# Row norms of the first block in one batch of four, weight maxima taken before the gain, constants emitted later

## The chip, the cores and the metric

The kernel runs on one core of a Trainium2 chip. The metric is the device time of one execution in microseconds (us), as the median of several runs. One profiled execution of the same kernel gives the trace that is read below.

Engine names: PE multiplies matrices, DVE is the vector engine, ACT the scalar engine (activations, copies with a scale), POOL the general engine, SP the queue from which all transfers are issued. Each engine works its instructions in a fixed order, one after the other, and waits where an operand isn't there.

## The reference, cut to what matters

```
h = rms_norm(x, norm_in)                    # x: 4096 and 1024 rows of 1024
z = h @ w_in                                # columns: Hyena 3*384 | q,k,v 3*384 | memory q 256 | gates 1024
u = short_conv3(z[:, :1152]); x0, x1, v = split(u); s = x1 * v
y_hyena = x0 * (long_conv(s, filter) + s * skip)
y_att   = dilated_attention(q, k, v)        # 6 heads, three windows
y_mem   = memory_attention(qm, mem)         # 4 heads, 256 memory rows, rms_norm(mem, mem_norm) @ w_mem_kv
x + (concat(y_hyena, y_att, y_mem) * silu(gates)) @ w_out
```

The gain `norm_in` is a factor per input column, so the kernel multiplies it into the rows of `w_in`, and `mem_norm` into the rows of the memory weights.

## The kernel before

**Numbers in two halves.** A float32 operand is split into a high half and a low half of 16 bits, and `mm3` (L278) makes one product of three matmuls: high by high, high by low, low by high. One product `zh` is 24 matmuls.

**Weights.** `wsplit` (L238) prepares a group of weight columns, 128 columns each: it loads a column tile `ws` (128x1024), multiplies it by the gain on POOL (L251), takes its largest absolute value on DVE (L252), spreads the maxima over the partitions (`peaks`, L222 to L229, small DVE steps), makes a power of two of them and its reciprocal `wsa` (L257 to L260), scales the tile into the high half on ACT (L263) and subtracts that from the scaled tile for the low half on DVE (L265, two pieces). The Hyena weights come in the groups (0), (3, 6), (1, 4, 7), (2, 5, 8), nine columns in six buffers; the weights of q, k, v and the memory queries come later in groups of 2, 2, 2, 2 and 3 columns in three buffers, while the Hyena products still run.

**Rows.** `norm_rows` (L350) loads four tiles `xt` of 128 rows, squares them on ACT with a running sum (L362), makes 1/sqrt of the mean for `batch` tiles at once (`nv` L364, `rsqrt` L205 to L209, with one step on ACT), scales each tile into its high half on ACT (L368) and makes the low half on DVE (L369). Four buffers hold the tiles. `prep_block` (L374) turns the halves into `hB`: block 0 by PE transposes (L385) with copies out by ACT (L389) and DVE (L387), later blocks by transfers that transpose (L381). `BATCH0 = 2` is the batch of block 0; later blocks take 4.

**The projection.** `hyena_proj` (L833) runs ten blocks of 512 rows, nine products each; two PSUM buffers hold `zh`. ACT copies each product out as `zb` (L879, two buffers) and makes `u` (L889), DVE adds two taps (L893), POOL multiplies x1 by v (L901). Block n+1 is normalised while the products of block n run. The generator `filters` is woven in: it emits `setup_late` (gains of the heads, their scales `gk`, `gsc`, `lsc`, the memory gain `g_mem`, the matrices `dft` and `cinv`), then the filter of the long convolution.

**What sets the order.** PE's order is the order of the code (`manual_schedule`, with the generators interleaved by due times). On ACT, DVE, POOL and SP a scheduler puts the instructions in order by priorities and modelled times, so an edit in one place can move what stands behind it there.

Of the kernel before, what the change touches and what calls it, by code (L numbers as in the profile page):

```python
# [12 lines left out]
F32 = mybir.dt.float32  # L13
# [9 lines left out]
P = 128  # L23
# [118 lines left out]
K_C, IDLE_1, IDLE_2, IDLE_3, IDLE_M = 1.35, (34000, 28000), (9000, 16000), 18000, 60000  # L142
K_A, IDLE_A, GATE_IDLE = 0.88, 20000, 0
LAG_I, WS_BUFS = 6, 6
MT, BATCH0 = 4, 2
MIX, K_Q = 0.1, 1.2
AHEAD = 2
XT, VLAG = 2, 4
# [33 lines left out]
class Layer:  # L182
# [52 lines left out]
            out=out.bitcast(I32), in_=m.bitcast(I32), scalar=0x7F800000, op=ALU.bitwise_and  # L235
        )

    def wsplit(self, pool, parts, S, gain=None, tag="ws", bufs=3):  # L238

        nc = self.nc
        n = len(parts)
        ws = []
        a = pool.tile([P, 4, 4], F32, tag=tag + "a", name="wsa", bufs=2)
        pk = self.peak(pool, tag)
        for j, (src, _, _) in enumerate(parts):
            w = pool.tile([P, KC, P], F32, tag=tag, name="ws", bufs=bufs)
            self.ld(w, src)
            if gain is not None:  # L250
                nc.gpsimd.tensor_tensor(out=w, in0=w, in1=gain.unsqueeze(2).to_broadcast([P, KC, P]), op=ALU.mult)  # L251
            nc.vector.tensor_reduce(  # L252
                out=pk[:, j:j + 1], in_=w, axis=AX.XY, op=ALU.max, apply_absolute_value=True
            )
            ws.append(w)
        pk = self.peaks(pool, pk, tag)
        nc.vector.tensor_scalar_max(a[:, 1, :n], pk[:, :n], 1e-30)  # L257
        self.pow2(a[:, 2, :n], a[:, 1, :n])
        nc.vector.tensor_scalar_mul(S, a[:, 2, :n], 1.0 / 16.0)
        nc.vector.reciprocal(a[:, 3, :n], S)  # L260
        for j, (_, dhi, dlo) in enumerate(parts):
            w = ws[j]
            nc.scalar.activation(out=dhi, in_=w, func=AF.Identity, scale=a[:, 3, j:j + 1])  # L263
            for k in range(0, KC, 4):
                nc.vector.scalar_tensor_tensor(  # L265
                    out=dlo[:, k:k + 4], in0=w[:, k:k + 4], scalar=a[:, 3, j:j + 1], in1=dhi[:, k:k + 4],
                    op0=ALU.mult, op1=ALU.subtract,
                )
# [19 lines left out]
    def setup(self):  # L288
        nc, c, x = self.nc, self.const, self.x
        self.ident = c.tile([P, P], F32, name="ident")  # L290
        make_identity(nc, self.ident)
        self.ident16 = c.tile([P, P], F16, name="ident16")
        nc.vector.tensor_copy(self.ident16, self.ident)
        self.ones = c.tile([P, P], F32, name="ones")
        nc.vector.memset(self.ones, 1.0)
        self.g_in = c.tile([P, KC], F32, name="g_in")
        self.ld(self.g_in, x["norm_in"][0].rearrange("(k p) -> p k", p=P))
        self.cinv = {}
        for i, (off, L) in enumerate(self.seqs):
            self.kmT[i] = c.tile([P, 2 * HM, NMEM], F16, name=f"kmT{i}")  # L300
            self.vm[i] = c.tile([P, 2, HM * E1 + HM * E], F16, name=f"vm{i}")
            self.rows[i] = self.dram.tile([L, ROW], F16, name=f"rows{i}")
            self.vrows[i] = self.dram.tile([L, VW], F16, name=f"vrows{i}")
            self.s_d[i] = self.dram.tile([3, P, L], F32, name=f"s_d{i}")
            self.x0_d[i] = self.dram.tile([3, P, L], F32, name=f"x0_d{i}")
            self.cv[i] = self.dram.tile([3, P, L], F32, name=f"cv{i}")
            NB = 2 * L // N1
            G = -(-65 // (P // (2 * NB)))
            self.as_d[i] = self.dram.tile([P, NB, 768], F16, name=f"as_d{i}")
            self.as_d[i, "k"] = self.dram.tile([P, NB, 768], F16, name=f"as_k{i}")  # L310
            self.bs[i] = self.dram.tile([P, G, 768], F16, name=f"bs{i}")
            self.yc[i] = [self.dram.tile([L, YW], F32, name=f"yc{i}_{j}") for j in range(3)]
            self.ym[i] = self.dram.tile([L, 256], F32, name=f"ym{i}")
            self.gt[i] = [self.dram.tile([P, KC, 512], F32, name=f"gt{i}_{b}") for b in range(L // 512)]
            for b in range(L // 512):
                self.hts[i, b] = self.dram.tile([P, 4, 16, P], F16, name=f"hts{i}_{b}")

    def setup_late(self):
        nc, c, x = self.nc, self.const, self.x
        self.g_mem = c.tile([P, KC], F32, name="g_mem")  # L320
        self.ld(self.g_mem, x["mem_norm"][0].rearrange("(k p) -> p k", p=P))
        self.S_v = c.tile([P, H], F32, name="S_v")
        self.S_mem = c.tile([P, 4], F32, name="S_mem")
        gains = c.tile([P, 4, E], F32, name="gains")
        for i, nm in enumerate(("att_q_norm", "att_k_norm", "mem_q_norm", "mem_k_norm")):
            self.ld(gains[:, i], x[nm][0].partition_broadcast(P))
        self.gk = c.tile([P, 2, E], F32, name="gk")
        nc.vector.tensor_tensor(out=self.gk, in0=gains[:, 0:4:2], in1=gains[:, 1:4:2], op=ALU.mult)
        a = c.tile([P, 2, 4], F32, name="gsc")
        for i in range(2):  # L330
            nc.vector.tensor_reduce(
                out=a[:, i, 0:1], in_=self.gk[:, i], axis=AX.X, op=ALU.max, apply_absolute_value=True
            )
        nc.vector.tensor_scalar_max(a[:, :, 0:1], a[:, :, 0:1], 1e-30)
        self.pow2(a[:, :, 1:2], a[:, :, 0:1])
        nc.vector.reciprocal(a[:, :, 2:3], a[:, :, 1:2])
        for i in range(2):
            nc.vector.tensor_scalar_mul(self.gk[:, i], self.gk[:, i], a[:, i, 2:3])
        self.lsc = c.tile([P, 2, 3], F32, name="lsc")
        nc.vector.tensor_scalar_mul(self.lsc[:, :, 0:1], a[:, :, 1:2], E ** -0.5)  # L340
        nc.vector.tensor_scalar_mul(self.lsc[:, :, 1:2], a[:, :, 2:3], E ** 0.5)
        nc.vector.tensor_scalar_mul(self.lsc[:, :, 2:3], a[:, :, 1:2], -(E ** -0.5))
        self.dft = c.tile([P, 4, P], F16, name="dft")
        self.ld(self.dft, x["dft"].rearrange("p (a b) -> p a b", a=4))
        for i in range(len(self.seqs)):
            self.cinv[i] = c.tile([P, 2, 64], F16, name=f"cinv{i}")
            self.ld(self.cinv[i], x[f"cinv{i}"].rearrange("p (a b) -> p a b", a=2))
# [1234 lines left out]
    def phases(self):  # L1582
# [9 lines left out]
        with self.pool("ps", PSUM) as ps:  # L1592
            with self.pool("p1") as pool:

                def filters():
                    yield IDLE_F
                    self.setup_late()
                    yield from scaled(sub(lambda p: self.hyena_filter(p, ps), "right"), K_F)
                    yield from scaled(sub(lambda p: self.bias_tables(p, ps), "right"), K_F)

                weave(tc, (self.hyena_proj(pool, ps), 2 * step), (filters(), step))
# [74 lines left out]
```

## Time and profile before

| | us |
|---|---|
| median of 3 runs | 3075.26 |
| lowest, highest | 3065.23, 3078.64 |
| the profiled execution | 3081.23 |
| its span | 3079.5 |
| PE busy | 2780.3 |
| DVE busy | 2072.2 |
| ACT busy | 1667.0 |
| POOL busy | 1338.5 |

The span is the time from the first to the last instruction that the trace shows; 1.73 us of the profiled execution lie around it. In a timeline row, the first number is the start in us from the start of the span, the second the duration; in brackets stands how long the engine was idle just before, and what ended that.

### The profile page before, as it was taken

The page shows a single profiled execution, that of the slowest core. Times are in us where ns is not written, and L with a number is a line of the kernel's source. Part 1 is how long each engine was busy: PE and PEld are TensorE (multiplying, and loading weights), DVE is VectorE, ACT ScalarE, POOL GpSimd, SP SyncE. Part 2 cuts the span into 40 slices and gives each one's busy share as a digit, 9 for nine tenths or more (in the row PEclk, how much of TensorE's full clock was granted, in tenths as well). Part 3 has the DMA queues.
Part 4 walks back from the last instruction along what each step waited for, and adds up shares of the span by engine and source line. Part 5 has one row for each costly group of instructions (what it writes and reads, how often), then busy time and mean ns, then how long its engine had stood idle before and what let it go on. Part 6 is the DMA issues. An engine that isn't in the chain of part 4 may idle for free. (4 is left out here: it accounts for less than half of the span.)

```text
span 3079.5 us, 55518 instructions
## 1 busy us (share of the span) xinstructions
PE 2780.3 (90%) x19620; PEld 1727.0 (56%) x19620; DVE 2072.2 (67%) x5239; ACT 1667.0 (54%) x3147; POOL 1338.5 (43%) x1574
## 2 busy tenths in 40 slices
PE   5998888988999997987998999998898899999999
PEld 2444444433544444543456666676666665778877
DVE  7777888788668761463668767676667666766663
ACT  5666666334779863472336666565565564323321
POOL 2336777243246651252424333333243344655551
PEclk9999999999999998998999999999999999999999
DMA  7654444545589866685589999998998979777762
GB/s 221 176 154 148 151 153 147 160 154 189 213 227 241 217 178 178 219 180 135 156 192 261 227 204 229 210 226 177 199 220 195 202 175 309 252 245 256 237 219 103
DMA packets 761953, 610.79 MB, mean 198 GB/s; under 512 B 514814, under 2 KB 702358, under 8 KB 758218
## 3 DMA queue, kind: packets, MB, share of 16 engines
q1 hardware_dynamic: 761674, 607.23, 73.4%
q8 instruction: 155, 2.54, 0.3%
q14 instruction: 124, 1.02, 0.1%
HBM read 289.08 MB, written 200.32 MB: 159 GB/s over the span
## 5 line engine op out<-in xcount | busy, mean ns | idle before, releaser
L1067 ACT ACTIVATE pt<-pt,nm 128x256 f32<-128x256 f32 (+2 forms) x880 | 349.8, 472 | 177.0 <-DVE nm L1065 170.2
L282 PE MATMUL z<-wA,hA 128*128 128x512 f16 (+1 forms) x960 | 353.9, 369 | 35.9 <-DVE vr L476 23.3
L284 PE MATMUL z<-wA,hA 128*128 128x512 f16 (+1 forms) x960 | 353.4, 368 | 0.0
L283 PE MATMUL z<-wA,hA 128*128 128x512 f16 (+1 forms) x960 | 353.1, 368 | 0.0
L1055 DVE CUSTOM_DVE_ANT_0 pt<-s,tab,lsc 128x256 f32<-128x256 f32 (+1 forms) x672 | 277.3, 448 | 84.6 <-PE s L1051 74.6
L282 PE MATMUL zh<-hB,wh 128*128 128x512 f16 x720 | 279.2, 388 | 24.4 <-ACT zb L879 24.2
L283 PE MATMUL zh<-hB,wh 128*128 128x512 f16 x720 | 278.8, 387 | 1.5 <-DVE hB L387 1.5
L284 PE MATMUL zh<-hB,wh 128*128 128x512 f16 x720 | 278.9, 387 | 0.0
L282 PE MATMUL oo<-wo,mhi 128*128 128x512 f32 x640 | 257.2, 402 | 8.9 <-ACT mhi L1531 3.6
L284 PE MATMUL oo<-wo,mlo 128*128 128x512 f32 x640 | 253.9, 397 | 0.3 <-POOL mlo L1532 0.3
L283 PE MATMUL oo<-wo,mhi 128*128 128x512 f32 x640 | 253.8, 396 | 0.0
L282 PE MATMUL zg<-hG,wg 128*128 128x512 f16 x640 | 246.0, 384 | 0.0
L284 PE MATMUL zg<-hG,wg 128*128 128x512 f16 x640 | 245.8, 384 | 0.0
L283 PE MATMUL zg<-hG,wg 128*128 128x512 f16 x640 | 245.7, 384 | 0.0
L1083 POOL CAST hl<-pt 128x256 f16<-128x256 f32 (+1 forms) x212 | 104.7, 508 | 312.0 <-ACT pt L1067 238.2
L1103 DVE TENSOR_TENSOR tl<-tt,th 128x512 f16<-128x512 f32 (+1 forms) x280 | 187.7, 672 | 56.7 <-ACT th L1102 55.2
L1102 ACT ACTIVATE th<-tt 128x512 f16<-128x512 f32 (+1 forms) x280 | 160.1, 574 | 115.0 <-PE yp L1124 55.0
L1048 PE MATMUL s<-kT,qT 128*128 128x256 f16 (+2 forms) x720 | 165.8, 261 | 42.0 <-DVE mx L1055 40.8
L1098 PE MATMUL tt<-ident,pt 128*128 128x128 f32 x1088 | 172.3, 280 | 31.3 <-DVE tl L1103 25.2
L1338 ACT ACTIVATE kt<-kp,rn 64x384 f32<-64x384 f32 x328 | 188.0, 573 | 12.8 <-PE kp L1332 7.6
L1084 POOL TENSOR_TENSOR hl<-pt,hl 128x256 f16<-128x256 f32 (+1 forms) x212 | 191.6, 911 | 6.8
L893 DVE SCALAR_TENSOR_TENSOR u<-zb,cw,u 128x512 f32<-128x512 f32 (+2 forms) x180 | 164.4, 917 | 30.4 <-ACT u L889 27.3
(303 smaller groups left out, 7217.1 us busy)
## 6 DMA issues: line engine op xcount, KB each, us to landing
y<-yc SPq DMA_DIRECT2D x120, 198.0 KB
yc<-y SPq DMA_DIRECT2D x112, 198.0 KB
xt<-in_x SPq DMA_DIRECT2D x40, 512.0 KB
hts<-hB SPq DMA_DIRECT2D x10, 2048.0 KB
hA<-hts SPq DMA_DIRECT2D x40, 512.0 KB
rows<-rw SPq DMA_DIRECT2D x40, 512.0 KB
hG<-hts SPq DMA_DIRECT2D x10, 2048.0 KB
gt<-go SPq DMA_DIRECT2D x80, 256.0 KB
```

The source lines that it names most:

```text
L282: nc.tensor.matmul(out, pick_l(lh, k), pick_r(rh, k), start=(k == 0), stop=False)
L283: nc.tensor.matmul(out, pick_l(lh, k), pick_r(rl, k), start=False, stop=False)
L284: nc.tensor.matmul(out, pick_l(ll, k), pick_r(rh, k), start=False, stop=(k == n - 1))
L893: nc.vector.scalar_tensor_tensor(out=u[:, :w], in0=zb[:, c0 + d:c1 + d], scalar=cw[:, j, tap:tap + 1], in1=u[:, :w], op0=ALU.mult, op1=ALU ...
L1048: nc.tensor.matmul(s[:, a, :W], g["qT"][:, h, qs], g["kT"][:, h, kc:kc + W], start=True, stop=False,)
L1055: nc.vector.tensor_tensor_reduce(out=pt[:, h, :W], in0=s[:, a, :W], in1=zero.to_broadcast([P, NMEM]) if mem else tb[:, h, t0:t0 + W], scal ...
L1067: nc.scalar.activation(out=pt[:, h, :W], in_=pt[:, h, :W], func=AF.Exp, bias=nm[:, h:h + 1])
L1084: nc.gpsimd.tensor_tensor(out=hl[:, 1, :, c], in0=src, in1=hl[:, 0, :, c], op=ALU.subtract)
L1098: nc.tensor.transpose(tt[:, a, ci, :], pt[:, 2 * pr + a, w0:w0 + P], self.ident)
L1102: nc.scalar.activation(out=th[:, :, :n], in_=tt[:, :, :n], func=AF.Copy)
L1103: nc.vector.tensor_tensor(out=tl[:, :, :n], in0=tt[:, :, :n], in1=th[:, :, :n], op=ALU.subtract)
L1338: nc.scalar.activation(out=kt[64 * b:64 * b + 64, a], in_=kp[64 * a:64 * a + 64, :DH], func=AF.Identity, scale=rn[64 * a:64 * a + 64, a * ...
```

## The change

`BATCH0` becomes 4: the four row tiles of block 0 share one reciprocal root. `wsplit` takes the maximum of the raw tile per input row (128x8 values), multiplies those by the absolute gain, takes the maximum of the eight, and only then has POOL multiply the tile by the gain, in place. `gain_of` loads a gain and makes its absolute value. `dft` is loaded where `setup_late` stood, and `setup_late` with the rest is emitted behind the filter.

```
-MT, BATCH0 = 4, 2
+MT, BATCH0 = 4, 4
...
             self.ld(w, src)
-            if gain is not None:
-                nc.gpsimd.tensor_tensor(out=w, in0=w, in1=gain.unsqueeze(2).to_broadcast([P, KC, P]), op=ALU.mult)
-            nc.vector.tensor_reduce(
-                out=pk[:, j:j + 1], in_=w, axis=AX.XY, op=ALU.max, apply_absolute_value=True
-            )
+            r = pool.tile([P, 2, KC], F32, tag=tag + "r", name="wsr", bufs=2)
+            nc.vector.tensor_reduce(out=r[:, 0], in_=w, axis=AX.X, op=ALU.max, apply_absolute_value=True)
+            nc.vector.tensor_tensor(out=r[:, 1], in0=r[:, 0], in1=gain[:, 1], op=ALU.mult)
+            nc.vector.tensor_reduce(out=pk[:, j:j + 1], in_=r[:, 1], axis=AX.X, op=ALU.max)
+            nc.gpsimd.tensor_tensor(out=w, in0=w, in1=gain[:, 0].unsqueeze(2).to_broadcast([P, KC, P]), op=ALU.mult)
...
-        self.g_in = c.tile([P, KC], F32, name="g_in")
-        self.ld(self.g_in, x["norm_in"][0].rearrange("(k p) -> p k", p=P))
+        self.g_in = self.gain_of("norm_in")
...
+    def gain_of(self, name):
+        g = self.const.tile([P, 2, KC], F32, name=name)
+        self.ld(g[:, 0], self.x[name][0].rearrange("(k p) -> p k", p=P))
+        self.nc.vector.scalar_tensor_tensor(
+            out=g[:, 1], in0=g[:, 0], scalar=-1.0, in1=g[:, 0], op0=ALU.mult, op1=ALU.max
+        )
+        return g
+
+    def setup_transforms(self):
+        nc, c, x = self.nc, self.const, self.x
+        self.dft = c.tile([P, 4, P], F16, name="dft")
+        self.ld(self.dft, x["dft"].rearrange("p (a b) -> p a b", a=4))
...
     def setup_late(self):
-        self.g_mem = c.tile([P, KC], F32, name="g_mem")
-        self.ld(self.g_mem, x["mem_norm"][0].rearrange("(k p) -> p k", p=P))
+        self.g_mem = self.gain_of("mem_norm")
...
-        self.dft = c.tile([P, 4, P], F16, name="dft")
-        self.ld(self.dft, x["dft"].rearrange("p (a b) -> p a b", a=4))
...
                     yield IDLE_F
+                    self.setup_transforms()
+                    yield from scaled(sub(lambda p: self.hyena_filter(p, ps), "right"), K_F)
                     self.setup_late()
-                    yield from scaled(sub(lambda p: self.hyena_filter(p, ps), "right"), K_F)
```

Behind the edit the lines stand 10 or 11 further down: L362, L368, L369 become L372, L378, L379; L387, L389 become L397, L399; L879, L889 become L889, L899.

PE's order is the same row by row. The other engines' orders differ in three stretches alone: at the start, while the later weights are split, and where the memory's keys and values are made.

DVE at the start (`xn` are row tiles, `rs_t` and `rs_y` the steps of the reciprocal root, `wsr` the eight maxima of a weight column). Before:

```order
L208 SCALAR_TENSOR_TENSOR rs_t<-rs_t,nv 128x2
L209 SCALAR_TENSOR_TENSOR rs_y<-rs_t,rs_y 128x2
L364 TENSOR_SCALAR nv<-nv 128x2
L205 RECIPROCAL rs_t<-nv 128x2
L265 SCALAR_TENSOR_TENSOR wh<-ws,wsa,wh 128x4x128 x2
L830 TENSOR_SCALAR cw<-cw,Sh_134 128x3
L369 SCALAR_TENSOR_TENSOR xn<-xt,rs_y,xn 128x1024
L252 TENSOR_REDUCE peak<-ws 128x1
L369 SCALAR_TENSOR_TENSOR xn<-xt,rs_y,xn 128x1024
L252 TENSOR_REDUCE peak<-ws 128x1 x2
L207 TENSOR_TENSOR rs_t<-rs_y 128x2
```

The same place on DVE in the changed kernel:

```order
L253 TENSOR_REDUCE peak<-wsr 128x1 x2
L251 TENSOR_REDUCE wsr<-ws 128x8
L207 TENSOR_TENSOR rs_t<-rs_y 128x4
L222 STREAM_TRANSPOSE peaks<-peak 128x32
L251 TENSOR_REDUCE wsr<-ws 128x8
L252 TENSOR_TENSOR wsr<-wsr,norm_in 128x8
L208 SCALAR_TENSOR_TENSOR rs_t<-rs_t,nv 128x4
L223 TENSOR_REDUCE peak<-peaks 128x1
L252 TENSOR_TENSOR wsr<-wsr,norm_in 128x8
L253 TENSOR_REDUCE peak<-wsr 128x1
L209 SCALAR_TENSOR_TENSOR rs_y<-rs_t,rs_y 128x4
```

Before, the root of the first two tiles (L209) stood ahead of the maxima of the second column and all later ones; now the one root of all four tiles stands behind the raw maxima (L251) of the first five columns.

ACT at the end of block 0 (`zb`, `u` leave a product; `xn,nv<-xt` squares a tile of block 2; the three L263 are the weights of the group (2, 5, 8)). Before:

```order
L879 ACTIVATE zb<-zh 128x512
L889 ACTIVATE u<-zb,cb,cw 128x511
L362 ACTIVATE xn,nv<-xt 128x1024
L263 ACTIVATE wh<-ws,wsa 128x8x128 x3
L879 ACTIVATE zb<-zh 128x512
```

The same place on ACT in the changed kernel:

```order
L889 ACTIVATE zb<-zh 128x512
L899 ACTIVATE u<-zb,cb,cw 128x511
L263 ACTIVATE wh<-ws,wsa 128x8x128 x3
L889 ACTIVATE zb<-zh 128x512
L899 ACTIVATE u<-zb,cb,cw 128x511
L372 ACTIVATE xn,nv<-xt 128x1024
```

The square, which waits for a load, moved from ahead of the three weight tiles to behind them and one more product.

ACT while the weights of q, k and v are split (`wA0` holds their high halves; here the second group of two columns; `zh_5343` before is the product `zh_5363` after). Before:

```order
L879 ACTIVATE zb_5368<-zh_5343 128x512
L263 ACTIVATE wA0_5838<-ws_5882,wsa_5879 128x8x128
L263 ACTIVATE wA0_5838<-ws_5886,wsa_5879 128x8x128
L879 ACTIVATE zb_5401<-zh_5376 128x512
L889 ACTIVATE u_5405<-zb_5401,cb_133,cw_132 128x511
```

The same place on ACT in the changed kernel:

```order
L263 ACTIVATE wA0_5858<-ws_5908,wsa_5905 128x8x128
L263 ACTIVATE wA0_5858<-ws_5915,wsa_5905 128x8x128
L889 ACTIVATE zb_5388<-zh_5363 128x512
L899 ACTIVATE u_5392<-zb_5388,cb_134,cw_133 128x511
L889 ACTIVATE zb_5421<-zh_5396 128x512
```

The two weight tiles now stand ahead of a product that left before them.

The small steps of `setup_late` on DVE (`gk`, `gsc`, `lsc`) and its loads on SP stay where they were to within some rows, among the first 75 rows of DVE.

## Rows read from the trace of the kernel before

**Rows 1.** The page: busy time by engine, the chain's shares, costliest groups.
```profile
PE 2780.3 (90%) x19620; PEld 1727.0 (56%) x19620; DVE 2072.2 (67%) x5239; ACT 1667.0 (54%) x3147; POOL 1338.5 (43%) x1574
...
PE 20%; DMA 11%; DVE 10%; issue 3%; ACT 2%; SPq 1%; POOL 1%; ACTq 0%; DVEq 0%; POOLq 0%
...
L282 PE MATMUL zh<-hB,wh 128*128 128x512 f16 x720 | 279.2, 388 | 24.4 <-ACT zb L879 24.2
```

**Rows 2.** Windows: stretch, length, busy time per engine, PE clock, DMA share, GB/s.
```profile
0.00:39.00 39.00, 7.83 (x65) 6.61 (x66) 29.07 (x82) 20.76 (x27) 15.04 (x19) 1.00 0.73 199
```

**Rows 3.** Timeline, 12 to 41 us: start, duration, engine, line, operation, [idle before <-releaser].
```profile
12.86 0.16 DVE L209 SCALAR_TENSOR_TENSOR rs_y<-rs_t,rs_y 128x2 f32<-128x2 f32 x1
...
18.03 1.27 DVE L369 SCALAR_TENSOR_TENSOR xn<-xt,rs_y,xn 128x1024 f16<-128x1024 f32 x1
19.58 1.90 POOL L251 TENSOR_TENSOR ws<-ws,g_in 128x1024 f32<-128x1024 f32 x1 [2.15 <-DMA ws<-in_w_in]
20.36 2.20 DVE L369 SCALAR_TENSOR_TENSOR xn<-xt,rs_y,xn 128x1024 f16<-128x1024 f32 x1
22.08 4.09 POOL L251 TENSOR_TENSOR ws<-ws,g_in 128x1024 f32<-128x1024 f32 x2 [0.60 <-DMA ws<-in_w_in]
26.89 0.29 DVE L328 TENSOR_TENSOR gk<-gains 128x128 f32<-128x128 f32 x1 [0.71 <-DMA gains<-in_mem_k_norm]
29.88 1.90 POOL L251 TENSOR_TENSOR ws<-ws,g_in 128x1024 f32<-128x1024 f32 x1 [3.72 <-DMA ws<-in_w_in]
31.05 1.06 ACT L362 ACTIVATE xn<-xt 128x1024 f32<-128x1024 f32 x1 [6.34 <-DMA xt<-in_x]
35.97 1.27 DVE L369 SCALAR_TENSOR_TENSOR xn<-xt,rs_y,xn 128x1024 f16<-128x1024 f32 x1
40.22 0.68 DVE L387 COPY hB<-xt 128x1024 f16<-128x1024 f16 x1
40.96 0.59 PE L283 MATMUL zh<-hB,wh 128*128 128x512 f16 x1 [1.47 <-DVE hB L387]
```

**Rows 4.** Timeline, 50 to 115 us: blocks 0 and 1 of the projection.
```profile
50.40 0.16 DVE L209 SCALAR_TENSOR_TENSOR rs_y<-rs_t,rs_y 128x4 f32<-128x4 f32 x1
51.88 3.75 POOL L251 TENSOR_TENSOR ws<-ws,g_in 128x1024 f32<-128x1024 f32 x2 [2.98 <-DMA ws<-in_w_in]
53.81 1.22 DVE L252 TENSOR_REDUCE peak<-ws 128x1 f32<-128x1024 f32 x1 [3.25 <-POOL ws L251]
68.69 0.17 DVE L260 RECIPROCAL wsa<-Sh 128x3 f32<-128x3 f32 x1
71.62 1.06 ACT L362 ACTIVATE xn<-xt 128x1024 f32<-128x1024 f32 x1 [6.46 <-DMA xt<-in_x]
72.67 3.21 ACT L263 ACTIVATE wh<-ws,wsa 128x1024 f16<-128x1024 f32 x3
76.42 0.38 PE L282 MATMUL zh<-hB,wh 128*128 128x512 f16 x1 [3.09 <-ACT zb L879]
101.02 1.06 ACT L362 ACTIVATE xn<-xt 128x1024 f32<-128x1024 f32 x1 [7.09 <-DMA hB<-xn]
104.55 0.38 PE L282 MATMUL zh<-hB,wh 128*128 128x512 f16 x1 [0.35 <-ACT zb L879]
114.29 0.38 PE L282 MATMUL zh<-hB,wh 128*128 128x512 f16 x1 [3.54 <-ACT zb L879]
```

**Rows 5.** Timeline, 614 to 670 us: later weights are split under the products.
```profile
614.98 0.60 ACT L879 ACTIVATE zb<-zh 128x512 f32<-128x512 f32 x1 [3.74 <-PE zh L284]
616.04 1.90 POOL L251 TENSOR_TENSOR ws<-ws,g_in 128x1024 f32<-128x1024 f32 x1 [7.68 <-DMA ws<-in_w_in]
625.99 2.19 ACT L263 ACTIVATE wA<-ws,wsa 128x1024 f16<-128x1024 f32 x2 [10.41 <-DVE wsa L260]
628.71 0.59 PE L282 MATMUL zh<-hB,wh 128*128 128x512 f16 x1 [3.45 <-ACT zb L879]
669.16 0.58 PE L282 MATMUL zh<-hB,wh 128*128 128x512 f16 x1 [3.83 <-ACT zb L879]
```

More of the change, by code (lines that the diff above doesn't have):

```diff
@@ L236, in pow2, with wsplit @@
         )
-    def wsplit(self, pool, parts, S, gain=None, tag="ws", bufs=3):
+    def wsplit(self, pool, parts, S, gain, tag="ws", bufs=3):
         nc = self.nc
```

## The prediction, made before the changed kernel ran

> **What bounds the kernel now.** I read the page first. PE is busy for 2780.3 of 3079.5 us, DVE for 2072.2, and the chain that ended last runs over PE more than over anything else [rows 1]. PE's order stays the same, so the change can win only where PE stands idle for something that the change moves. There are two such places. The first is the start: in the first 39 us PE works 7.83 us and is idle for 31 [rows 2]. The second is the projection: over its 720 products' first matmuls PE waited 24.4 us in all, 24.2 of them for ACT to copy out an earlier product [rows 1]. So the whole prize behind the start is below 25 us, and only the part of it that lies where orders differ (the timeline shows 3.09, 0.35, 3.54, 3.45 and 3.83 us [rows 4, 5], together 14.3) is within reach. Then I read the timelines of these places, at each asking what ended ACT's or DVE's wait. Half a per cent of the median, 15.4 us, is about what a measurement of this kernel can tell from no change.
>
> **The start.** Before, the root of tiles 0 and 1 is done at 13.0 us, that of tiles 2 and 3 comes later because ACT first squares a tile of block 1 and waits 6.34 us for its load, until 31.05 [rows 3]. The projection runs in earnest from 40.96, when its second matmul gets the copy that DVE makes at 40.22 of the last tile's low half; that low half is done at 35.97 + 1.27 = 37.24, so 3.7 us lie between [rows 3]. After, the square of block 1 stands behind the four scales and that wait is gone for them, but DVE's root of all four tiles stands behind the raw maxima of five weight columns. The fifth column is there at 22.08, when POOL starts on two columns after waiting for a transfer [rows 3]. A whole-tile maximum takes 1.22 us [rows 4]; five small steps and the last one of the root, 0.16 each like the step at 12.86 [rows 3], make 1.0. The root is done at 22.08 + 1.22 + 1.0 = 24.3. Four scales at 1.06 each (a square of the same tile costs that [rows 3]) end at 28.6. The first low half stands behind `gk`, which waits for its load until 26.89 [rows 3]. The other three stand behind the maximum of the seventh column, which lands at 29.88 [rows 3]: 29.88 + 1.22 = 31.1. Three low halves and some 0.5 us of small steps between them give 31.1 + 3 x 1.27 + 0.5 = 35.4 at the shorter duration, 31.1 + 3 x 2.20 + 0.5 = 38.2 at the longer one [rows 3]. With the 3.7 us behind them the second matmul starts between 39.1 and 41.9; before it was 40.96. The ends are -1.9 and +0.9; I take -0.5, the middle, since POOL has one or two multiplications to lay beside three low halves.
>
> Which duration a low half has is decided by POOL: the one at 18.03, with POOL waiting, took 1.27 us, the one that began at 20.36 inside POOL's multiplication of 19.58 to 21.48 took 2.20 [rows 3]. The Trainium skill, page "SBUF — State Buffer", section "Who interferes with whom", says why: a DVE instruction with two inputs in SBUF contends with a GpSimd instruction that reads SBUF, and the later one is blocked fully. The trace agrees within 0.2 us (blocked until 21.48, the low half would have ended at 22.75; it ended at 22.56). By that rule this change has a cost that its text hides: POOL's multiplication used to begin at the load and now begins when DVE's maximum ends, which is just when DVE goes on to a low half. That is rival D.
>
> **The end of block 0.** PE waited 3.09 us at 76.42 for ACT's `zb` [rows 4]. That `zb` stood behind three weight tiles (3.21 us), these behind a square that waited 6.46 us for its load until 71.62 [rows 4]. The reciprocal that the weight tiles need was done at 68.86 [rows 4], while ACT stood waiting. After, they stand ahead of the square: 68.86 + 3.21 = 72.1, and with 0.6 for the copy 72.7, before PE ran out of buffers at 76.42 - 3.09 = 73.33. So the 3.09 us go: -3.1. If the reciprocal is made later by over 0.6 us, part of it stays; the other end is 0.
>
> **Block 1.** Its root, done at 50.56 before [rows 4], now stands behind the raw maxima of the eighth and ninth column. POOL started on these two at 51.88, after a wait for a transfer, and took 3.75 us [rows 4], so the ninth is there by 53.8 and the root comes at 53.8 + 1.22 + 1.0 = 56.0, 5.4 us later. Part of that was hidden, because the low halves waited on DVE behind those two columns anyway; I pass on half, 2.5 us. These low halves free the tile buffers, so block 2's loads come 2.5 us later, then its transposing transfers, and with them the square of block 3 that waited 7.09 us until 101.02 [rows 4]. Behind it on ACT stands the `zb` for which PE waited at 104.55. PE's idle time there was 0.35 us [rows 4], so PE is just at the edge: this is a point paced by transfers, and what PE won before it (0.5 + 3.1 us) is lost there again if the transfers don't come earlier, and 2.5 us more. So far +2.5 by the count at 104.55, with ends -3.6 (the transfers come as much earlier as PE) and +2.5 + 0.9. Behind it the squares stand more thinly between the products (one, then one, then two, where one and two stood ahead of a single `zb`), and PE's 3.54 us at 114.29 [rows 4] go in part: I take -2.5, ends -3.5 and 0. By 140 us the sum is 0, with ends -7.1 and +3.4.
>
> **The weights of q, k and v.** POOL's 1.90 us (616.04 [rows 5]) leave the chain from load to maximum, two small steps of 0.16 us (bounds 0.13 to 0.29, the latter from `gk` [rows 3]) and the longer wait for both columns enter; high halves of a group start some 1 us earlier than 625.99 [rows 5], at 625.0. But in ACT's order the second group now stands ahead of the product that ACT copied at 614.98 [rows 5]. This product is stuck until 625.0 + 2.19 = 627.2, and PE, whose two buffers fill one product of 5.2 us earlier (its buffers ran out at 628.71 - 3.45 = 625.3 before), stops at 620.1 and goes on at 627.8 as its first matmul follows the copy by 0.6 us: 7.8 us instead of 3.45, +4.4. The next groups are paced by their loads into three buffers, and PE has a similar wait of 3.83 us at 669.16 [rows 5] in which a late PE catches up. I take +1 for the stretch: of the 4.4 most is regained. Ends: -2.8, if both waits shorten by 1.4 us and nothing is held, and +6.3, if the 4.4 stay and the fourth group, whose three tiles also stand ahead of a copy now, adds its 1.9 us of a third tile and reciprocal.
>
> **The rest.** 20 weight columns in these two stretches and the memory's columns cost DVE two small steps each, 0.3 us a column. DVE works 75% of the start and isn't what PE waits for elsewhere: 0; if it were all on the path at the start, it is in the 24.3 above. The move of `setup_late` leaves its DVE steps and loads almost where they were, ahead of the products; worth 0, and at most the 0.71 us for which `gk` waited [rows 3] either way. In the memory stage some rows trade places; 0, ends -1 and +1.
>
> **The sum.** 0 by 140 us, +1 in the weights, 0 behind it: +1, ends -11 and +11. The profiled execution's 3081.23 us would become 3082; it lies 6 us or 0.2% above the median of 3075.26, which would become 3076. I put the forecast at 3075: the +1 is smaller than any of its terms.
>
> **The rivals.** *B, the gains stay.* The transfers of block 2 come earlier with PE, so 101.02 is no fixed point; then -1.9 at the start, -3.1, -3.5 and -2.8 hold: -11.3, 3064. For it: POOL's 1.90 us leave every chain, and the wait on ACT ahead of block 0's second half is gone. Against it: DVE's root of block 1 is behind two more weight columns. *C, slower by ACT's place.* Each of the four later groups of q, k, v weights stands one product earlier on ACT, and none of the 4.4 us is regained: 4 x 4.4 = 17.6, so 3093. It decides where a group's reciprocal comes later than 5.2 us (one product) after the copy that it holds is due; the second group's comes 10.4 us after (ACT's wait ahead of 625.99 [rows 5]). Against it: only for two groups does the order show a copy that is held. *D, the start grows by POOL beside DVE.* All three late low halves at 2.20 and `gk`, the reductions and the last copy delayed too: the second matmul at 42 to 43, +2; with the rest as above 3077. *E, the change doesn't do what it says.* The constants don't move later, so nothing is won by it; that is already in the sum at 0 and gives the forecast's time.
>
> **How the numbers follow.** Forecast (with E) 0.70, B 0.14, C 0.06, D 0.10. Faster by over 0.5% (below 3060) needs B with more than I can find: half of B's chance, 0.07, and a little from the forecast's end of -11: 0.08 in all. Slower by over 0.5% (above 3090.6) is C, 0.06, and the end of +11 with the unexplained: 0.07. Within 0.5%: 0.85. The range takes in the forecast's ends -11 and +11, D and B, with some us for the spread of the three runs (3065 to 3079): 3060 to 3088, and leaves out C.
>
> **What would show it.** In the profile after: a root for four tiles at about 24 and a second matmul at 39 to 42 us; no wait of PE at the end of block 0; a wait of PE of some 5 us near 101 to 107 for a `zb` behind a square; a wait of about 8 us near 628, and a shorter one behind it. From the q, k, v products on, each step a constant shift from before. It is wrong if the wait near 101 is absent (then B), if waits of 4 us and more stand behind each of the four groups (then C), or if the stretches behind 700 us, where the order is the same, change in length.

## The result and the profile after

The changed kernel takes 3094.32 us (median of 6 runs, 3087.8 to 3102.17) beside 3076.17 us for the kernel before; the ratio is 1.006 with a 95% interval of 1.004 to 1.008. It is 18 us slower. The profiled execution is the slowest of the six, 3102.17 us. In the experiments below, two executions far above all others (9971 us of e6, 3512 us of the kernel before) are left out of the ratios. The prediction was 3075 us, no change, within 3060 to 3088, and held a slowdown of over 0.5% for unlikely (0.07). The measured time lies 6 us above the range.

The page of the changed kernel shows no engine that is much busier. Beside [rows 1], PE's busy time is almost the same (6 us more), DVE has 26 us more, and PE's wait for `zb` at the first matmuls of products grew from 24.2 to 31.0 us. That is 7 us and not 18, so PE must wait longer elsewhere too:

```profile
PE 2786.3 (90%) x19620; PEld 1728.5 (56%) x19620; DVE 2098.5 (68%) x5300; ACT 1666.7 (54%) x3146; POOL 1346.0 (43%) x1574
...
L282 PE MATMUL zh<-hB,wh 128*128 128x512 f16 x720 | 280.5, 390 | 31.3 <-ACT zb L889 31.0
```

PE's order is the same in both kernels, so the n-th matmul of one can be laid beside the n-th of the other, and the program cut at the same matmuls. The windows below are cut so: the start until the middle of block 1, the middle of the projection, the split of the q, k, v and gate weights under the last products, the long convolution, and the rest. Columns: stretch, length, busy time of PE, PEld, DVE, ACT, POOL, PE clock, DMA share, GB/s. First the kernel before:

```profile
0.00:123.91 123.91, 82.56 (x385) 39.38 (x386) 93.28 (x207) 78.62 (x107) 35.92 (x52) 0.99 0.79 221
123.91:556.72 432.81, 387.04 (x1796) 181.71 (x1796) 349.68 (x500) 275.57 (x484) 282.01 (x323) 0.97 0.47 145
556.72:804.44 247.72, 220.52 (x1038) 103.74 (x1038) 192.25 (x477) 94.89 (x143) 78.41 (x94) 0.95 0.57 176
804.44:1443.43 638.99, 557.57 (x3491) 302.93 (x3492) 359.59 (x673) 413.83 (x768) 268.71 (x264) 0.96 0.73 200
1443.43:3074.79 1631.36, 1532.23 (x12912) 1099.20 (x12911) 1076.76 (x3384) 804.09 (x1648) 673.47 (x842) 0.98 0.84 214
```

The same stretches of the changed kernel:

```profile
0.00:132.27 132.27, 85.79 (x384) 40.06 (x385) 97.82 (x219) 73.04 (x100) 43.59 (x55) 0.96 0.72 204
132.27:564.29 432.02, 384.57 (x1798) 180.92 (x1797) 350.18 (x504) 280.83 (x490) 279.69 (x321) 0.97 0.47 146
564.29:825.08 260.79, 219.94 (x1039) 103.69 (x1039) 205.90 (x517) 95.55 (x144) 82.55 (x94) 0.93 0.54 170
825.08:1454.17 629.09, 555.45 (x3492) 302.52 (x3492) 358.62 (x671) 413.03 (x767) 269.26 (x264) 0.96 0.70 202
1454.17:3095.41 1641.24, 1540.13 (x12911) 1101.31 (x12911) 1085.26 (x3392) 804.25 (x1648) 670.90 (x842) 0.98 0.83 212
```

Two stretches grew where the orders differ: the start by 8.4 us and the split by 13.1 us. Between them the length stays (-0.8). The last two stretches (-9.9, +9.9) are not read as effects of the change: over the 19 kernels of this study with the same order on PE they lie between 628 and 645 us and between 1619 and 1641 us, up and down by some 10 us in single executions. The third place where the orders differ, the memory's keys and values, lies there, and its share can't be told from this spread. Where less than 10 us is asked, the medians decide.

**The start.** PE and ACT in the changed kernel (timeline: start, duration, operation, [idle before <- what ended it]):

```profile
41.26 0.58 PE L283 MATMUL zh<-hB,wh 128*128 128x512 f16 x1 [1.18 <-DVE hB L397]
94.94 0.21 ACT L206 ACTIVATE rs_y<-rs_t 128x4 f32<-128x4 f32 x1 [5.22 <-DVE rs_t L205]
95.69 0.38 PE L282 MATMUL zh<-hB,wh 128*128 128x512 f16 x1 [3.35 <-ACT zb L889]
106.74 1.06 ACT L372 ACTIVATE xn<-xt 128x1024 f32<-128x1024 f32 x1 [3.84 <-DMA hB<-xn]
114.38 0.61 ACT L645 ACTIVATE dec<-delta,tneg 128x384 f32<-128x384 f32 x1 [3.14 <-DMA delta<-in_delta]
120.52 0.81 ACT L899 ACTIVATE u<-zb,cb,cw 128x512 f32<-128x512 f32 x1 [2.86 <-DMA s_d<-u]
122.53 1.06 ACT L372 ACTIVATE xn<-xt 128x1024 f32<-128x1024 f32 x1 [1.20 <-DMA xt<-in_x]
125.67 1.22 PE L685 MATMUL p<-h,fw 128*128 128x512 f32 x1 [5.86 <-ACT h L666]
```

The second matmul comes at 41.26, 0.3 us later than in [rows 3]. Of the wait of 3.09 us at the end of block 0 [rows 4] 0.29 us are left, about as forecast. Then PE waits at 95.69 for a `zb` that stands on ACT behind a step of block 2's root, for which ACT itself waited 5.22 us. The last row is one that the prediction doesn't have: the filter's matmul waits 5.86 us for a sine on ACT. Ahead of the sine stand two squares, `dec` and a `u`, and each of these waited for a transfer; the last two of these waits end at 120.52 and 122.53, while PE stands idle (from 119.81 on).

**The split of the later weights.** DVE, POOL, ACT and PE at the second group of q, k, v columns, the place of [rows 5]:

```profile
622.94 1.22 DVE L251 TENSOR_REDUCE wsr<-ws 128x8 f32<-128x1024 f32 x1 [5.85 <-DMA ws<-in_w_in]
624.08 0.74 DVE L903 SCALAR_TENSOR_TENSOR u<-zb,cw,u 128x511 f32<-128x511 f32 x1
624.24 2.33 POOL L254 TENSOR_TENSOR ws<-ws,norm_in 128x1024 f32<-128x1024 f32 x1 [6.77 <-DVE wsr L251]
624.73 1.86 DVE L252 TENSOR_TENSOR wsr<-wsr,norm_in 128x8 f32<-128x8 f32 x1
627.80 2.33 POOL L254 TENSOR_TENSOR ws<-ws,norm_in 128x1024 f32<-128x1024 f32 x1 [1.23 <-DVE wsr L251]
628.37 1.78 DVE L252 TENSOR_TENSOR wsr<-wsr,norm_in 128x8 f32<-128x8 f32 x1
634.97 2.19 ACT L263 ACTIVATE wA<-ws,wsa 128x1024 f16<-128x1024 f32 x2 [15.84 <-DVE wsa L260]
637.68 0.58 PE L282 MATMUL zh<-hB,wh 128*128 128x512 f16 x1 [9.73 <-ACT zb L889]
681.66 0.58 PE L282 MATMUL zh<-hB,wh 128*128 128x512 f16 x1 [5.17 <-ACT zb L889]
702.46 0.38 PE L282 MATMUL zh<-hB,wh 128*128 128x512 f16 x1 [2.52 <-ACT zb L889]
732.16 0.48 PE L282 MATMUL z<-wA,hA 128*128 128x384 f16 x1 [8.81 <-ACT zs L451]
```

ACT stood 15.84 us in front of two high halves, with the product that [rows 5] shows leaving ahead of them now stuck behind. From the first use of the group's first column to its high halves the kernel before took 625.99 - 616.04 = 10.0 us [rows 5], the changed one 634.97 - 622.94 = 12.0 us: longer, though POOL's multiplication is off the path to the maximum. The two L252 rows say why. The multiplication of eight maxima by the gain, 128x8 values, took 1.86 and 1.78 us. It ended at 626.59 and 630.15, within 0.02 us of the end of POOL's multiplication of the whole tile (626.57, 630.13). POOL starts that one 0.08 us after the maximum of the raw tile; on DVE a tap (L903, the second row) stands between the maximum and the small step, so that the small step begins inside POOL's multiplication and ends with it. In the whole trace 14 of the 28 small steps begin inside an instruction of POOL; each ends 0.02 us after that instruction, and the other 14 took 0.13 to 0.17 us. By lines, the small step took over all its instances (count | busy, mean ns):

```profile
L252 DVE TENSOR_TENSOR wsr<-wsr,norm_in 128x8 f32<-128x8 f32 x28 | 22.4, 803 | 0.1
```

PE's waits in the split, of the kernel before and then of the changed one (what waited, for what: us in all, times, longest):

```profile
PE zh L282 <- ACT zb L879: 9.8, 3, 3.8
PE z L282 <- ACT zs L441: 9.5, 5, 3.5
PE z L282 <- DVE vr L476: 2.3, 3, 0.8
```
```profile
PE zh L282 <- ACT zb L889: 17.4, 3, 9.7
PE z L282 <- ACT zs L451: 11.8, 3, 8.8
PE z L282 <- DVE vr L486: 8.0, 2, 6.2
```

About half of the new waiting is at products whose `zb` is held, the other half at the first q, k, v tiles, behind the last products.

### The profile page after: what moved, and what is told of

Same layout as the page of the kernel before. It is cut to its first block, busy times and chain, and to the rows that moved or that the text cites. A ratio compares the mean times of both kernels' runs of the same rounds, so it can differ in the third digit from the quotient of the medians.

```text
span 3100.0 us, 55591 instructions
## 1 busy us (share of the span) xinstructions
PE 2786.3 (90%) x19620; PEld 1728.5 (56%) x19620; DVE 2098.5 (68%) x5300; ACT 1666.7 (54%) x3146; POOL 1346.0 (43%) x1574
## 5 line engine op out<-in xcount | busy, mean ns | idle before, releaser
L903 DVE SCALAR_TENSOR_TENSOR u<-zb,cw,u 128x512 f32<-128x512 f32 (+2 forms) x180 | 164.5, 915 | 33.2 <-ACT u L899 28.2
```

The source lines that it names most:

```text
L903: nc.vector.scalar_tensor_tensor(out=u[:, :w], in0=zb[:, c0 + d:c1 + d], scalar=cw[:, j, tap:tap + 1], in1=u[:, :w], op0=ALU.mult, op1=ALU ...
```

## The experiments

Each ratio is to the kernel before, run in turn with it on the same chip, with its 95% interval; it can differ by 0.1% from the quotient of two medians. Windows are cut at the same two matmuls as the split above (247.72 us before, 260.79 changed).

**Which of the three edits.** The theory (A: the raw maxima) and its rivals (B: the batch, C: the late constants) are told in the expectations, as are A1 and A2, O and M further on. One edit of the change at a time (e1 to e3), the change without the raw maxima (e6):

```
e1  -MT, BATCH0 = 4, 2                e2  the change, with  -MT, BATCH0 = 4, 4
    +MT, BATCH0 = 4, 4                                      +MT, BATCH0 = 4, 2
                                          and setup_late where it was
e3  setup_transforms ahead of the     e6  the change, with the multiplication by the gain
    filter, setup_late behind it          and one maximum, as before
```

> Only the batch of four: the kernel before with BATCH0 = 4, maxima still taken behind POOL's multiplication, constants where they were. Theory A (the raw maxima cost the time: the small multiplication by the absolute gain, 128x8, stands on DVE behind the start of POOL's multiplication of the same column and took 0.80 us in the mean, up to 1.87, where 0.16 was counted; and ACT's order moved with it): within 4 us of before. Theory B (the batch and its late roots cost it, by way of block 1): 8 to 15 us slower than before, with PE's shift of 8 us against before at 140 us already there. Theory C (emitting the constants later costs it, by ACT's wait for the filter's inputs near 114 us): same as before.

> Only the raw maxima: the changed kernel with BATCH0 = 2 and the constants emitted where they were before. Theory A: 10 to 18 us slower than before, and a wait of PE of 7 to 10 us behind the second group of q, k, v weights. Theory B: at most 5 us slower. Theory C: at most 5 us slower.

> Only the late constants: the kernel before with dft loaded ahead of the filter and the rest of setup_late behind it. Theory A and B: within 4 us of before. Theory C: 5 to 10 us slower, with PE waiting 4 to 6 us near 115 to 125 us for ACT's first sine of the filter.

> The changed kernel with the maxima taken as before: the batch of four and the late constants together. Theories A1 and A2: the sum of the two single edits, 2 to 10 us slower than before, all of it in PE's shift by 140 us, and no further shift between 560 and 800 us. If instead the three edits need each other, it is slower by over 12 us.

| kernel | median us | ratio | interval |
|---|---|---|---|
| e1, batch of four | 3080.09 | 1.0019 | 1.0004 to 1.0034 |
| e2, raw maxima | 3093.67 | 1.0063 | 1.0038 to 1.0089 |
| e3, late constants | 3077.55 | 1.0005 | 0.9987 to 1.0024 |
| e6, batch and late constants | 3073.76 | 0.9998 | 0.9983 to 1.0013 |

The raw maxima alone make the whole loss; the other two edits together cost nothing. In e2 PE waits 11 us behind the second group, a little more than expected. Two expectations miss: e1 alone is 6 us slower (1 to 10), between what A and B said, and e6 was to be 2 to 10 us slower. The late start of e6, 131.65 us against 123.91 to the same matmul, with the same wait for a sine, does not show in its median; why it costs nothing there stays open. The batch of four by itself starts the second matmul 5.5 us earlier (35.4 us) and has lost that again by 124 us, where the filter's matmul waits 7.52 us for ACT. A try to keep this gain, by weaving the filter in later, failed:

```
-IDLE_F, K_F, C_FFN = 50000, 2.4, 2000
+IDLE_F, K_F, C_FFN = 70000, 2.4, 2000
```

> The batch of four alone, with the filter's first matmuls woven in 20 us of PE time later (its start time 70000 in place of 50000 ns), so that its sines don't stand on ACT while block 2 is made. If the batch's gain at the start (the second matmul 5.5 us earlier) was lost to ACT's wait of 7.5 us near 122 us for the filter, that wait is gone and PE's shift at 140 us is 0 to -5 us: the kernel is as fast as before or up to 6 us faster. If block 2's transfers are what took it back, the wait stands at a product instead, and the shift is the same +5 us as with the batch alone.

It is 1.0046 (1.0028 to 1.0064) of before, 3086.73 us. The wait stands at a product instead of at the filter, as the second half of the expectation has it, and moving the filter moved the order of the later weights too:

```profile
121.77 0.59 PE L282 MATMUL zh<-hB,wh 128*128 128x512 f16 x1 [6.72 <-ACT zb L879]
```

**Steps or order, first attempts.** Small steps without the early start (f1), early start without small steps (f2), and the small multiplication on POOL (e4):

```
f1  nc.gpsimd.tensor_tensor(out=w, ...)           # POOL first, as before
    reduce 128x8; multiply by ones 128x8; reduce 128x1
f2  nc.vector.tensor_reduce(out=pk[:, j:j + 1], in_=w, axis=AX.XY, ...)   # raw tile, gain left out
    nc.gpsimd.tensor_tensor(out=w, ...)
e4  -nc.vector.tensor_tensor(out=r[:, 1], in0=r[:, 0], in1=gain[:, 1], op=ALU.mult)
    +nc.gpsimd.tensor_tensor(out=r[:, 1], in0=r[:, 0], in1=gain[:, 1], op=ALU.mult)
```

> The kernel before with the maxima taken in three steps (128x8, times one, 128x1) but still behind POOL's multiplication: all the small steps of the change, none of the early start. On ACT the second group of q, k, v weights stands where it stood before, behind the product that the change lets it hold. Theory A1 (the steps themselves cost the time: two more per column, the small multiplication up to 1.9 us beside POOL): 10 to 18 us slower than before, like the raw maxima alone. Theory A2 (the places that the scheduler gives to the weights' instructions on ACT and DVE cost it, because a maximum that no longer stands behind POOL looks ready earlier than the transfer delivers it): within 5 us of before, and PE's wait behind the second group at most 4 us.

> The kernel before with the maximum taken on the raw tile in one step, without any small step; the gain is left out of the maximum, which only chooses a power of two. On ACT the second group of q, k, v weights stands ahead of the product that it held in the changed kernel. Theory A1: as fast as before or faster, by up to 8 us, since POOL's 1.9 us a column leave the chain and nothing is added. Theory A2: 6 to 16 us slower than before, with a wait of PE of 6 to 9 us behind the second group and others behind the last ones, though the chain from a column's landing to its high half is some 2 us shorter than in the changed kernel.

> The changed kernel with one edit: the multiplication of the eight maxima by the absolute gain is on POOL, ahead of the large multiplication, where no other instruction of POOL can run beside it. Theory A: the time from a column's landing to its group's high halves falls by 2 us or more in the q, k, v groups, and the kernel is 5 to 15 us faster than the changed one. Theories B and C: within 4 us of the changed kernel.

f1 is 1.0020 (1.0005 to 1.0036) of before, f2 1.0059 (1.0040 to 1.0077), e4 1.0054 (1.0034 to 1.0074). f1 and f2 speak for the order (A2), but f1 says little of a step beside POOL: half of its 32 small steps took 0.16 us or less. e4 misses its expectation: it is no faster than the changed kernel. Its windows say that its two places go apart: the split shrank to 250.15 us, while its start took 132.65 us, 8.7 more than before.

```profile
568.64:818.79 250.15, 217.89 (x1039) 103.57 (x1039) 198.88 (x498) 95.34 (x144) 86.89 (x113) 0.95 0.57 177
```

Then ACT's high halves in f2 (p1), these and DVE's maxima (p2), and both in the changed kernel itself (p4), were kept behind the products and taps that they stood behind before:

```
+with self.tc.issue_after(<the zb of product 70, 76, 79, 83 or 87>):      # p1, p2, p4
     nc.scalar.activation(out=dhi, in_=w, func=AF.Identity, ...)
+with self.tc.issue_after(<the tap that it stood behind>):                # p2, p4
     nc.vector.tensor_reduce(...)
```

> The kernel with the one-step raw maximum (gain left out of the maximum) and one order edit: ACT's high halves of each group of q, k, v weights may not be issued before the product that they stood behind in the kernel before. DVE's order stays that of the raw maximum. If ACT's place alone makes the loss (theory A2 in its narrow form): within 5 us of before, the wait of PE behind the second group at most 4 us. If DVE's maxima, which now stand ahead of taps and wait there for transfers, make it: 8 us or more slower, as without the pin.

> The same with DVE's raw maxima pinned too, those of q, k, v and of the gates: each stands behind the tap that its multiplied maximum stood behind in the kernel before. Theory A2: within 4 us of before, at best some us faster, since POOL's 1.9 us a column are off the chain in the order of before. If the order isn't the cause, 10 us slower as before the pin.

> The changed kernel itself, all three edits and all small steps, with both pins (ACT's high halves and DVE's raw maxima of the q, k, v and gate weights kept behind the products and taps of the kernel before). Theory A2: 10 to 16 us faster than the changed kernel, within 6 us of before, and no further shift of PE between 560 and 800 us but 2 to 4 us for the longer chain. Theory A1 (the steps, at up to 1.9 us): at most 4 us faster than the changed kernel.

They are 1.0076 (1.0063 to 1.0089), 1.0051 (1.0037 to 1.0065) and 1.0067 (1.0051 to 1.0082) of before: all three miss what A2 expected, and come out as the other branch of each expectation has it. Only in p2 did the pins take away what they were for: the wait right behind the second group, 6.65 us in f2, is 0.84 us, with 2.24 one product later. In p1 and p4 it is still 5.58 and 5.18 us. f2, then the two rows of p2:

```profile
632.92 0.59 PE L281 MATMUL zh<-hB,wh 128*128 128x512 f16 x1 [6.65 <-ACT zb L889]
```
```profile
632.06 0.38 PE L286 MATMUL zh<-hB,wh 128*128 128x512 f16 x1 [0.84 <-ACT zb L897]
639.64 0.38 PE L286 MATMUL zh<-hB,wh 128*128 128x512 f16 x1 [2.24 <-ACT zb L897]
```

But PE of p2, 2 us behind the kernel before at the matmul of 669.16 [rows 5], was 15 us behind some 70 us later. In its narrow form, a single product held by two high halves, the theory falls: to take that wait away gives nothing back.

**Steps or order, crossed.** s1 swaps two statements: the maximum first, then POOL's multiplication (the gain is left out of the maximum). It has the same instructions as before, so that the whole order of one can be imposed on the other: s2 is the swap in the order of before, s3 is before in the order of the swap, on ACT, DVE and SP (PE's is the same).

```
s1  -nc.gpsimd.tensor_tensor(out=w, ...)          s2, s3
    -nc.vector.tensor_reduce(out=pk[:, j:j + 1], ...)   +for a, b in zip(order, order[1:]):
    +nc.vector.tensor_reduce(out=pk[:, j:j + 1], ...)   +    tc.add_manual_dep(here[b], a, NoSync)
    +nc.gpsimd.tensor_tensor(out=w, ...)
```

> The kernel before with two statements swapped: the maximum of a weight column first, on the raw tile in one step, then POOL's multiplication (the gain is left out of the maximum, which only chooses a power of two). The same instructions as before, in the order that the scheduler makes of them. Both theories left, O (the order in which the four engines stand, on SP too) and M (POOL's multiplication behind the maximum, and what it meets there), expect it 10 to 18 us slower than before, as with the one-step raw maximum measured earlier.

> The same swap, but ACT, DVE, SP and PE held, instruction by instruction, to the order of the kernel before; only POOL's multiplications move, each behind its maximum. Theory O: within 4 us of before, or some us faster, since POOL's 1.9 us a column have left the chain to the maximum. Theory M: 8 to 18 us slower than before.

> The kernel before, with POOL's multiplication ahead of the maximum as ever, but ACT, DVE, SP and PE held to the order that the scheduler made for the swap. Theory O: 8 to 20 us slower than before. Theory M: within 5 us of before.

| | order of before | order of the swap |
|---|---|---|
| multiplication, then maximum | 1 (3074.48 us) | s3: 1.0111 (1.0091 to 1.0130) |
| maximum, then multiplication | s2: 1.0003 (0.9990 to 1.0015) | s1: 1.0089 (1.0068 to 1.0111) |

The order carries the loss, whichever way the maximum is taken; the swap itself is worth 0 in one order and a gain of 0.2%, inside the intervals, in the other. s2 came out as O had it; s1 and s3 lost more than expected, 27 and 34 us. The windows of the split, of s1, s2 and s3 in turn, show it in one execution each (247.72 us before):

```profile
562.61:820.79 258.18, 220.89 (x1039) 104.33 (x1039) 200.49 (x480) 95.11 (x144) 83.89 (x94) 0.93 0.55 171
```
```profile
557.06:803.63 246.57, 219.81 (x1039) 103.90 (x1038) 197.38 (x477) 95.07 (x143) 79.77 (x94) 0.95 0.57 178
```
```profile
565.83:829.39 263.56, 223.88 (x1039) 105.13 (x1038) 186.97 (x480) 95.35 (x144) 80.41 (x94) 0.93 0.53 168
```

s3 has the least DVE work of the three and is the slowest: DVE's busy time is not the cause. To place the loss, s8 holds the swap to the order of before at the start alone, s9 from the middle of the projection on:

```
s8  order = order of before, up to some 300 us      s9  order = order of before, from there on
```

> The swap of maximum and multiplication with ACT, DVE and SP held to the order of before at the start alone (up to some 300 us), free behind it. By the shifts of PE in the traces of the swap (6 us by 557 us, 10 more by 804) it is 5 to 8 us faster than the free swap, 16 to 22 us slower than before.

> The swap with the order of before held from some 300 us on alone, and the start free: the split of the q, k, v and gate weights stands as before. By the same shifts it is 15 to 22 us faster than the free swap and 3 to 8 us slower than before.

s8 is 1.0060 (1.0042 to 1.0078), s9 1.0019 (1.0004 to 1.0035). Both are as expected beside the kernel before. The start's order costs 0.2 to 0.3%, the order at the split 0.6 to 0.7%. Which engine's order it is stays open: no run holds one engine alone.

**The changed kernel itself in the order of before.** a1 holds all instructions that both kernels have (over 99%); a4 does the same and has the small multiplication on POOL.

```
a1  the change, +tc.add_manual_dep(...) along the order of before
a4  a1 with  -nc.vector.tensor_tensor(out=r[:, 1], ...)
             +nc.gpsimd.tensor_tensor(out=r[:, 1], ...)
```

> The changed kernel itself, all three edits and all small steps, with ACT, DVE and SP held to the order of the kernel before in every instruction that both have (over 99% of them); the new small steps, the batch's root and what has no partner stand where the scheduler puts them between. If the order is the whole cause of the 18 us: within 4 us of before. What is left above that is what the small steps cost in themselves, the multiplication by the gain beside POOL above all (28 times 0.80 us on DVE in the changed kernel): up to 8 us.

> The same, with the multiplication of the eight maxima by the absolute gain on POOL. If the small multiplication beside POOL still costs something in the order of before, this is 2 to 6 us faster than the changed kernel held to that order, and at best some us faster than before; if not, it is the same.

a1 is 1.0038 (1.0023 to 1.0053) of before, a4 0.9987 (0.9974 to 1.0000): 3098.01 and 3082.3 us beside 3085.55. So the small step costs 0.5% even in the order of before, and on POOL it costs nothing that can be measured. Both expectations had it smaller: a1 was to be at most 8 us slower than before and is 12, a4 2 to 6 us faster than a1 and is 16. The small step of a1, then of a4, by lines (idle time in the last column), and then the windows of their splits:

```profile
L260 DVE TENSOR_TENSOR wsr<-wsr,norm_in 128x8 f32<-128x8 f32 x28 | 20.3, 726 | 0.2
```
```profile
L260 POOL TENSOR_TENSOR wsr<-wsr,norm_in 128x8 f32<-128x8 f32 x28 | 12.4, 443 | 77.8 <-DVE wsr L259 63.8 <-DVE wsa L268 7.7 <-DVE peak L261 3.8
```
```profile
561.79:819.37 257.58, 222.91 (x1039) 104.75 (x1038) 211.08 (x515) 94.94 (x143) 81.10 (x94) 0.94 0.56 170
```
```profile
557.01:805.91 248.90, 222.29 (x1039) 104.33 (x1038) 201.66 (x497) 95.04 (x144) 86.09 (x113) 0.95 0.57 176
```

The four forms of the change, ratio and length of the split in one execution (247.72 us before):

| | small step on DVE | small step on POOL |
|---|---|---|
| order that the scheduler made | the change: 1.006, 260.79 us | e4: 1.0054, 250.15 us |
| order of before | a1: 1.0038, 257.58 us | a4: 0.9987, 248.90 us |

What is shown, then: the raw maxima bring two causes, and in the time of the whole kernel it takes both out to get the loss back. The order: the one that the scheduler made for the swap costs 10 to 16 us at the split wherever it stands (258.18, 263.56), and nothing of that is left in the order of before (246.57). The small step beside POOL: 8.7 us at the split in the order of before (a1 against a4), and 3.4 at the start. How the two share the 13.1 us of the changed kernel's split is not shown. There the small step seems to weigh more: with the order taken out 9.9 us of them are left (a1), with the step moved 2.4 (e4, whose order on ACT has the q, k, v groups behind the same products as the changed kernel). In e4's trace most of the loss stands in the start, 8.7 us; e6 lost 7.7 there and was not slower, so that part stays open. a4 is the fastest version of the change, 0.7% ahead of it on the ratios, and no more than 0.3% ahead of the kernel before.

## Why the prediction was wrong, point by point

- **The bound**: PE's waits on ACT in the projection were one of the places, and as a bound on what can be won it stands. What can be lost has no such bound, and the range leaned on it. Half of what was lost at the split, and the 5.86 us at the filter, stand at matmuls that the 24.4 us don't count.
- **The start** was right: the root at 24.3 us (measured 25.0), the second matmul at 39.1 to 41.9 (41.26), so that -0.5 was +0.3.
- **The end of block 0**: the wait of 3.09 us went to 0.29, about as said. But PE was 1.3 us behind just ahead of it (72.69 against 71.44 us), where +0.3 stood at the start, so it came out only 1.5 us ahead of the kernel before.
- **Block 1** failed. "I pass on half, 2.5 us" of a root 5.4 us late: the root was done at 59.2 us, 8.7 late; 1.7 of the 3.2 us more are its own last step, priced 0.16 us, which took 1.85 beside POOL. At the matmul of 104.55 PE was 4.9 us late and not 2.5. The -2.5 behind it came out with the wrong sign, since PE waits 5.86 us there for the filter's sine on ACT, and no step of the sum had it. 0 by 140 us was +8.4.
- **The split** failed at the term that decides, +1 in the sum and 13.1 us in the trace. Of the "two small steps of 0.16 us (bounds 0.13 to 0.29)" the multiplication took 0.80 us in the mean, and 1.86 and 1.78 at the second group. The prediction itself quoted, for the low halves, the rule of the Trainium skill (page "SBUF — State Buffer", section "Who interferes with whom") by which a DVE step with two SBUF inputs is blocked by a POOL step that reads SBUF. The rows above (ends within 0.02 us) agree with the rule. The prediction applied it to the long low halves and not to the new small step, which has two SBUF inputs as well and begins behind POOL's start. So the chain grew by 2 us where -1 was forecast. a4 confirms the step: with it on POOL the split takes 248.90 us instead of 257.58.
- **"Of the 4.4 most is regained"** failed. PE is 7.6 us behind the kernel before where the split begins, 16.5 at the matmul of 628.71, behind the held product, and 12.5 at 669.16: 4 us were regained. Then it was lost again at the last products and the first q, k, v tiles, and at the end of the split PE is 20.6 us behind, 13.1 more than at its beginning. p2 shows the same with the first wait taken out. That the order of all engines is worth more than one held copy was in no term of the sum.
- **Rival C** had the right time, 3093, and its place, with a chance of 0.06. The time is in part luck, as its mechanism, 4.4 us at each of four later groups, is not what the trace shows. The high halves of the five groups stood on ACT behind 71, 77, 80, 84 and 88 copies `zb` before, and stand behind 72, 76, 80, 83 and 86 after: three groups hold a copy, and not two, as the prediction says against C, or four. PE's waits at these three are 9.73, 5.17 and 2.52 us.

## What to carry to other kernels

Where a scheduler sets the order, a change of a few instructions is a change of the whole order, and at a tight place that can be worth more than what the instructions cost: here 1.1% with not one instruction changed. Cross the two, new work in the old order and old work in the new, before a cause is named; here, holding a few groups of instructions was not enough. And a step is not cheap because it is small: price it beside what the other engines do at that moment (here 1.8 us in place of 0.16 beside POOL), above all if the change itself starts that work just ahead of it.

## What the runs showed of the hardware that was not expected

A multiplication of 128x8 values on DVE, 0.13 us at its shortest, took up to 1.87 us where it began inside an instruction of POOL, and 0.80 us in the mean over 28; on POOL, ahead of the multiplication of the 128x1024 tile, it took 0.44 us in the mean. One step of the reciprocal root (128x4) went from 0.16 to 1.85 us in the same way.
